# A second MLP product from fourteen block products a chunk instead of seven and four direct units

## The chip, the core and the metric

The kernel runs on one core of a Trainium2 chip. The metric is the device time of one execution in microseconds. All arithmetic is float32: each operand of a matmul is split into a high part (`wh`, rounded to the matmul's format) and a low part (`wl`, the rest), and a product of two matrices is three matmuls: high times high, high times low, low times high. The engines are TensorE (PE, with its weight loads PEld), VectorE (DVE), ScalarE (ACT), GpSimd (POOL) and SyncE (SP, which issues most transfers).

## The reference

Two residual layers over 256 positions of width 2048: the first mixes with a state-space scan, the second with a dilated attention; after each comes an MLP of width 8192:

```
def sq_relu_mlp(h, w1, w2):
    a = jax.nn.relu(h @ w1)
    return (a * a) @ w2
...
        x = x + sq_relu_mlp(rms_norm(x, norm_mlp[i]), mlp_w1[i], mlp_w2[i])
```

Here h is 256 x 2048, w1 is 2048 x 8192 and w2 is 8192 x 2048. The change touches only how `(a * a) @ w2` is computed.

## The kernel before

Every weight goes through the same three steps (`fetch`, L157): a transfer of 1 MB (128 x 2048 float32) into a buffer `raw`, a copy by ScalarE that rounds it to `wh` (L187), and a subtraction by VectorE that leaves `wl` (L188). Such a block is a unit. `unit_plan` (L47) lists all units in the order in which TensorE uses them, and `take` (L192) fetches two units ahead, since there are three buffers each of `raw`, `wh` and `wl`. In the MLP a unit's split is issued behind that of the unit before it (L178), so VectorE and ScalarE split in the plan's order. Each engine runs its own queue in order; a scheduler that works on its own estimate of time decides how the splits, the emptying of PSUM and the rest are interleaved on VectorE and ScalarE.

The MLP (`mlp`, L752) runs over the width 8192 in 8 chunks of 1024. In a chunk there are 8 U units of the first product: 32 matmuls each, half of them 512 and half 256 columns wide. A U unit ends in one PSUM bank and is emptied by `evacuate` (L773): ScalarE copies one half of the bank, VectorE adds the other (`cols_sum`, L235; in the trace the tile h_0t for U0, h_1t for U1), applies relu and the row factor (L777), ScalarE squares it and makes the high part, VectorE the low part.

While the U units of chunk c + 1 run, the second product of chunk c is worked off. Its left operand is 256 x 1024, seen as 2 x 2 blocks a11, a12 (the first 128 positions), a21, a22; its right one is 1024 x 2048. The columns of the result are four blocks of 512, j = 0 to 3. For j = 0 and 1 the 2 x 2 block product is made from seven products instead of eight (P1 to P7, Winograd's form): `combine` (L782) makes four combinations of the a blocks, and the weight blocks are combined by transfers that accumulate, which GpSimd issues (L176): they add the next block to the buffer `wa` or `wb` in place, once the split before has read it. A product is 12 matmuls of 512 columns (L812). It ends in a bank x, w or z, and VectorE adds that bank to the residual `x_res` or subtracts it (L818), with the running sums in the banks, so that seven products give all four blocks. For j = 2 and 3 the product is made directly, in four D units of 24 matmuls each (`rows_unit`, L238).

The order of a chunk is written by hand (L69):

```
CHUNK_ORDER = ("U0 U1 P1 U2 P2 U3 U4 P5 D20 D21 P3 U5 U6 P6 U7 D30 P7 D31 P4").split()
```

U and D units share four PSUM banks in turn, the products and small work the four others. Chunk 7 has no U units beside it and is multiplied directly.

Of the kernel before, what the change touches and what calls it, by code (L numbers as in the profile page):

```python
# [14 lines left out]
P = 128  # L15
S = 256
# [22 lines left out]
LOOKAHEAD = 3  # L39
# [7 lines left out]
def unit_plan():  # L47
# [21 lines left out]
CHUNK_ORDER = ("U0 U1 P1 U2 P2 U3 U4 P5 D20 D21 P3 U5 U6 P6 U7 D30 P7 D31 P4").split()  # L69
# [10 lines left out]
def mlp_plan(layer):  # L80
    plan = [("w1", layer, 0, u) for u in range(8)]
    for c in range(FC):
        if c + 1 < FC:
            for item in CHUNK_ORDER:
                if item[0] == "U":
                    plan.append(("w1", layer, c + 1, int(item[1])))
                elif item[0] == "P":
                    plan.append(("w2", layer, c, item))
                else:
                    plan.append(("w2", layer, c, int(item[1]), int(item[2])))  # L90
        else:
            plan += [("w2", layer, c, j, q) for j in range(4) for q in range(2)]
    return plan
# [3 lines left out]
def hybrid_trunk_kernel(ctx: ExitStack, tc: tile.TileContext, a: dict, out: bass.AP):  # L97
# [7 lines left out]

    def mm_bank(name):
        return psum.tile([P, 512], F32, tag="mm", name=name, bufs=4)

    def sm_bank(name):
        return psum.tile([P, 512], F32, tag="sm", name=name, bufs=4)  # L110
# [24 lines left out]
    def source(u):  # L135
        kind = u[0]
        if kind == "in":
            return a["w_in"][u[1] * 10 + u[2]], 2048
        if kind == "dt":
            return a["w_dt"], 2048  # L140
        if kind == "out":
            return a["w_out"][u[1] * 4 + u[2]], 2048
        if kind == "qk":
            return a["w_qk"][u[1] * 6 + u[2]], 2048
        if kind == "v":
            return a["w_v"][u[1] * 4 + u[2]], 1536
        if kind == "o":
            return a["w_o"][u[1] * 4 + u[2]], 2048
        if kind == "w1":
            return a["w1"][(u[1] * FC + u[2]) * 8 + u[3]], 2048  # L150
        if len(u) == 4:
            q, j = WINOGRAD[u[3]][1:3]
        else:
            j, q = u[3:]
        return a["w2"][((u[1] * FC + u[2]) * 4 + j) * 2 + q], 2048

    def fetch(i, ends=(16,)):  # L157

        src, n = source(plan[i])
        product = plan[i][3] if plan[i][0] == "w2" and len(plan[i]) == 4 else None  # L160
        where, _, _, begins = WINOGRAD.get(product, ("raw", 0, 0, True))
        if where == "raw":
            raw = wts.tile([P, 2048], F32, tag="raw", name=f"raw{i}", bufs=3)
        elif begins:
            raw = sums_of[where] = mlp_pool[0].tile([P, 2048], F32, tag=where, name=f"{where}{i}", bufs=1)
        else:
            raw = sums_of[where]
        wh = wts.tile([P, 2048], F32R, tag="wh", name=f"wh{i}", bufs=3)
        wl = wts.tile([P, 2048], F32R, tag="wl", name=f"wl{i}", bufs=3)
        ready[i] = (wh, wl)  # L170
        for k0, k1 in zip((0, *ends), ends):
            c = slice(k0 * n // 16, k1 * n // 16)
            if begins:
                load[i] = nc.sync.dma_start(raw[:, c], src[:, c]).ins
            else:
                nc.gpsimd.dma_start(raw[:, c], src[:, c], accum_op=ALU.add)  # L176
            with ExitStack() as order:
# [3 lines left out]
                if product == "P4":  # L181
# [10 lines left out]
    def take(*u):  # L192
# [3 lines left out]
        while cursor[1] < min(len(plan), i + LOOKAHEAD):  # L196
# [5 lines left out]
    def cols_units(us, xs, names, cuts=(), first=False, between=None):  # L202
# [3 lines left out]
        banks = [mm_bank(name) for name in names]  # L206
# [545 lines left out]
    def mlp(layer, pool, xn, done):  # L752
# [9 lines left out]
        mlp_pool[0] = pool  # L762

# [4 lines left out]
        def chunk(c):  # L768
            act = pool.tile([P, 8, 2, S], F32R, tag="act", name=f"act{layer}_{c}", bufs=2)
            r = pool.tile([P, 8, S], F32, tag="r", name=f"r{layer}_{c}", bufs=1)  # L770
            return act, r

        def evacuate(c, u, ps, act, r):  # L773
            name = f"h{layer}_{c}_{u}"
            tot = cols_sum(ps, name)
            t = r[:, u]
            nc.vector.scalar_tensor_tensor(t, tot, 0.0, rb, op0=ALU.max, op1=ALU.mult)  # L777
            nc.scalar.activation(t, t, AF.Square)  # L778
            nc.scalar.activation(act[:, u, 0, :], t, AF.Copy)
            nc.vector.tensor_tensor(act[:, u, 1, :], t, act[:, u, 0, :].bitcast(F32), ALU.subtract)  # L780

        def combine(c, r):  # L782

            t1, t2 = slice(0, P), slice(P, S)
            a11, a12, a21, a22 = r[:, :4, t1], r[:, 4:, t1], r[:, :4, t2], r[:, 4:, t2]
            s = [pool.tile([P, 4, P], F32, tag="s", name=f"s{layer}_{c}_{k}", bufs=2) for k in range(2)]
            parts = {}

            def split(k, t):
                parts[k] = pool.tile([P, 4, 2, P], F32R, tag=f"s{k}", name=f"sp{layer}_{c}_{k}", bufs=1)  # L790
                nc.scalar.activation(parts[k][:, :, 0], t, AF.Copy)
                nc.vector.tensor_tensor(parts[k][:, :, 1], t, parts[k][:, :, 0].bitcast(F32), ALU.subtract)

            nc.vector.tensor_tensor(s[0], a21, a22, ALU.subtract)
            split(1, s[0])
            nc.vector.scalar_tensor_tensor(s[1], s[0], -1.0, a11, op0=ALU.mult, op1=ALU.subtract)
            split(2, s[1])
            s4 = pool.tile([P, 4, P], F32, tag="s", name=f"s{layer}_{c}_3", bufs=2)
            nc.vector.scalar_tensor_tensor(s4, a12, -1.0, s[1], op0=ALU.mult, op1=ALU.subtract)
            split(4, s4)  # L800
            s3 = pool.tile([P, 4, P], F32, tag="s", name=f"s{layer}_{c}_2", bufs=2)
            nc.vector.tensor_tensor(s3, a11, a21, ALU.add)
            split(3, s3)
            return parts
# [11 lines left out]
        def put(m, j, ps, op):  # L816
            xc = x_res[:, m, j * 512:(j + 1) * 512]
            nc.vector.tensor_tensor(xc, xc, ps, op)  # L818

        act, r = chunk(0)  # L820
        us, names = [("w1", layer, 0, u) for u in range(8)], [f"h{layer}_0_{u}" for u in range(8)]
        for u, ps in enumerate(cols_many(us, xs, names)):
            evacuate(0, u, ps, act, r)

        for c in range(FC - 1):
            parts = combine(c, r)
            act_next, r_next = chunk(c + 1)
            banks = {}

            def half(k0, t):  # L830
                return lambda i, part: act[:, k0 + i, part, t]

            t1, t2 = slice(0, P), slice(P, S)
            of = {"P1": half(0, t1), "P2": half(4, t1), "P4": half(4, t2)}
            for k, item in ((1, "P5"), (2, "P6"), (3, "P7"), (4, "P3")):
                of[item] = lambda i, part, k=k: parts[k][:, i, part]
            lhs = lambda k, part, t: act[:, k, part, t]
            for item in CHUNK_ORDER:
                if item[0] == "U":
                    u = int(item[1])  # L840
                    ps = in_order(lambda: cols_units([("w1", layer, c + 1, u)], xs,
                                                     [f"h{layer}_{c + 1}_{u}"], first=(u == 0))[0])
                    evacuate(c + 1, u, ps, act_next, r_next)
                elif item[0] == "D":
                    j, q = int(item[1]), int(item[2])
                    if q == 0:
                        banks[j] = [mm_bank(f"d{layer}_{c}_{j}_{m}") for m in range(NH)]
                    in_order(lambda: rows_unit(banks[j], [("w2", layer, c, j, q)], lhs, 4 * q, 4, 512,
                                               q == 0, q == 1))
                    if q == 1:  # L850
                        add_residual(banks[j], j)
                else:
                    where = {"P1": "x", "P6": "x", "P7": "x", "P4": "x", "P5": "w", "P3": "w",
                             "P2": "z"}[item]
                    first = where not in banks
                    if first:
                        banks[where] = sm_bank(f"p{where}{layer}_{c}")
                    product(c, item, banks[where], of[item], first)
                    for m, j, op in {"P1": [(0, 0, ALU.add)], "P2": [(0, 0, ALU.add)],
                                     "P5": [(1, 1, ALU.add)], "P3": [(0, 1, ALU.subtract)],  # L860
                                     "P6": [(0, 1, ALU.subtract)], "P7": [(1, 1, ALU.add)],
                                     "P4": [(1, 0, ALU.subtract)]}[item]:
                        put(m, j, banks[where], op)
            act, r = act_next, r_next

        c = FC - 1
        lhs = lambda k, part, t: act[:, k, part, t]
# [18 lines left out]
    with tc.tile_pool(name="mlp1", bufs=1) as pool:  # L886
# [5 lines left out]
        def gained(j):  # L892
            if j == 0:
                fin.append(pool.tile([P, D], F32, tag="wb", name="fin", bufs=1))
# [116 lines left out]
```

## Time and profile before

| | |
|---|---|
| median of 3 runs | 2602.84 us (2599.51 to 2604.07) |
| the profiled execution | 2599.4 us |
| its span | 2597.6 us |
| MLP of the first layer | about 675 to 1386 us of the span |
| MLP of the second layer | about 1905 us to the end |
| PE, DVE, ACT busy over the span | 99%, 72%, 56% |
| mean moved by DMA | 206 GB/s |

Times of single instructions come from the profiled execution. Instructions that follow each other on an engine overlap a little in the records, so the sum of their durations is more than the time that they occupy. A line such as `wl<-raw,wh 128x2048 ... x13 | 29.8, 2291` is a group: what is written from what, the shape, how many, their busy time in us, and the mean of one in ns; behind the next bar stands how long the engine sat idle before them, and what ended that. In the list of a stretch by engines the columns are named in the text.

### The profile page before, as it was taken

Reading aid. Unit: us, or ns where it says so; the run is one execution under the profiler, and the core shown is the slowest. Engines: PE = TensorE matmul, PEld = TensorE weight load, DVE = VectorE, ACT = ScalarE, POOL = GpSimd, SP = SyncE. Lnnn points to the kernel's source line nnn. Section 1 sums busy time; section 2 is a strip of 40 time slices with the busy share of each in tenths; the row PEclk is TensorE's granted clock in tenths of the full one; section 3 lists DMA queues with packets and bytes.
Section 4 is the critical chain, followed back from the end, with each engine's and each line's share of the span. In section 5 each row is a group of like instructions: output and inputs, shape, how many; then the busy total and the mean of one; then the engine's idle time right before and its main releaser. Section 6 shows DMA issues by size and latency. Waiting matters only on the chain.

```text
span 2597.6 us, 34416 instructions
## 1 busy us (share of the span) xinstructions
PE 2582.3 (99%) x13977; PEld 2211.8 (85%) x13977; DVE 1878.7 (72%) x2182; ACT 1459.1 (56%) x1774; POOL 160.0 (6%) x131
## 2 busy tenths in 40 slices
PE   9999999999999999999999999999999999999998
PEld 7888888888888888888888999998888888888887
DVE  7888688686677677777766666666667777677765
ACT  7675365464555555555546655656565555555554
POOL 0121021211000000000000000000000000000001
PEclk9999999999999999999999999999999999999999
DMA  7645555555577787778765454444457777877783
GB/s 284 209 169 193 191 195 180 180 191 187 191 222 232 236 231 239 229 235 234 231 195 183 166 175 162 159 158 165 168 209 216 234 237 235 232 230 239 228 241 131
DMA packets 79087, 533.88 MB, mean 206 GB/s; under 512 B 8784, under 2 KB 9424, under 8 KB 19536
## 3 DMA queue, kind: packets, MB, share of 16 engines
q1 hardware_dynamic: 68256, 462.86, 50.5%
q0 software_dynamic: 8064, 58.72, 12.5%
q10 hardware_dynamic: 2608, 10.09, 1.2%
q8 instruction: 110, 1.80, 0.3%
q14 instruction: 49, 0.40, 0.0%
HBM read 529.48 MB, written 2.16 MB: 205 GB/s over the span
## 4 chain that ended last, share of the span: by engine, by line
PE 95%; DVE 2%; ACT 1%; DMA 1%; POOL 1%; issue 1%; SPq 0%; ACTq 0%; POOLq 0%; DVEq 0%
PE h L215 28%; PE qk L215 10%; PE c L215 8%; PE px L812 6%; PE d L249 5%; PE d L250 5%; PE d L251 5%; PE pw L812 3%; PE wo L250 2%; PE wo L249 2%; PE wo L251 2%; PE z L250 2%; PE z L251 2%; PE z L249 2%; PE v L249 2%; PE v L251 2%
## 5 line engine op out<-in xcount | busy, mean ns | idle before, releaser
L188 DVE TENSOR_TENSOR wl<-raw,wh 128x2048 fp32r<-128x2048 f32 (+4 forms) x428 | 934.6, 2185 | 578.0 <-ACT wh L187 577.0
L187 ACT ACTIVATE wh<-raw 128x2048 fp32r<-128x2048 f32 (+4 forms) x428 | 782.7, 1831 | 640.8 <-PE h L215 216.5
L215 PE MATMUL h<-xn,wh 128*128 128x512 f32 x2048 | 715.9, 394 | 0.0
L215 PE MATMUL h<-xn,wl 128*128 128x256 f32 x2048 | 571.2, 280 | 0.0
L215 PEld LDWEIGHTS h<-xn,wh 128*128 128x128 f32 x2048 | 383.9, 188 | 87.0
L215 PEld LDWEIGHTS h<-xn,wl 128*128 128x128 f32 x2048 | 383.6, 187 | 4.2
L215 PE MATMUL c<-xn,wh 128*128 128x512 f32 x768 | 272.4, 397 | 2.5 <-ACT wh L187 2.3
L215 PE MATMUL qk<-xn,wh 128*128 128x512 f32 x768 | 271.1, 395 | 0.0
L251 PE MATMUL d<-wh,act 128*128 128x512 f32 x576 | 224.3, 390 | 0.0
L250 PE MATMUL d<-wl,act 128*128 128x512 f32 x576 | 223.9, 389 | 0.0
L249 PE MATMUL d<-wh,act 128*128 128x512 f32 x576 | 218.7, 390 | 0.0
L215 PE MATMUL qk<-xn,wl 128*128 128x256 f32 x768 | 216.7, 284 | 0.0
L215 PE MATMUL c<-xn,wl 128*128 128x256 f32 x768 | 215.0, 282 | 0.8 <-DVE wl L188 0.8
L215 PEld LDWEIGHTS c<-xn,wh 128*128 128x128 f32 x768 | 143.7, 188 | 37.2 <-ACT wh L187 4.4
L215 PEld LDWEIGHTS qk<-xn,wh 128*128 128x128 f32 x768 | 143.9, 188 | 30.2
L215 PEld LDWEIGHTS c<-xn,wl 128*128 128x128 f32 x768 | 143.9, 188 | 3.0 <-DVE wl L188 1.1
L215 PEld LDWEIGHTS qk<-xn,wl 128*128 128x128 f32 x768 | 143.7, 188 | 3.2 <-issue 2.7
L251 PEld LDWEIGHTS d<-wh,act 128*128 128x128 f32 x576 | 108.1, 188 | 22.6
L249 PEld LDWEIGHTS d<-wh,act 128*128 128x128 f32 x576 | 108.1, 188 | 22.3
L250 PEld LDWEIGHTS d<-wl,act 128*128 128x128 f32 x576 | 108.1, 188 | 22.0
L778 ACT ACTIVATE r<-r 128x256 f32<-128x256 f32 x128 | 52.2, 410 | 101.7 <-DVE r L777 101.7
L250 PE MATMUL z<-wl,xn 128*128 128x512 f32 x256 | 101.4, 396 | 0.3 <-DVE wl L188 0.3
(348 smaller groups left out, 4186.3 us busy)
## 6 DMA issues: line engine op xcount, KB each, us to landing
raw<-in_w SPq DMA_DIRECT2D x214, 1024.0 KB, 4.9
raw<-in_w_in SPq DMA_DIRECT2D x74, 1024.0 KB, 4.8
raw<-in_w_qk SPq DMA_DIRECT2D x48, 1024.0 KB, 4.8
wa<-in_w POOLq DMA_DIRECT2D x42, 1024.0 KB, 8.2
raw<-in_w_out SPq DMA_DIRECT2D x32, 1024.0 KB, 4.8
raw<-in_w_v SPq DMA_DIRECT2D x32, 768.0 KB, 4.3
wa<-in_w SPq DMA_DIRECT2D x14, 1024.0 KB, 4.8
wb<-in_w SPq DMA_DIRECT2D x14, 1024.0 KB, 5.0
```

The costliest lines, as they stand in the source:

```text
L187: high[i] = nc.scalar.activation(wh[:, c], raw[:, c], AF.Copy).ins
L188: low[i] = nc.vector.tensor_tensor(wl[:, c], raw[:, c], wh[:, c].bitcast(F32), ALU.subtract).ins
L215: latest[0] = nc.tensor.matmul(ps[:, :n], (wh, wl)[part][:, kt * P:(kt + 1) * P], xs[:, kt, :, :].rearrange("p a t -> p (a t)")[:, :n], st ...
L249: nc.tensor.matmul(banks[m][:, :n], hi, wh[:, c], start=st, stop=False)
L250: nc.tensor.matmul(banks[m][:, :n], hi, wl[:, c], start=False, stop=False)
L251: latest[0] = nc.tensor.matmul(banks[m][:, :n], lo, wh[:, c], start=False, stop=sp).ins
L778: nc.scalar.activation(t, t, AF.Square)
L812: latest[0] = nc.tensor.matmul(ps, lhs(i, part), w[:, n], start=(first and i == 0 and part == 0 and w is wh), stop=(i == 3 and part == 1), ...
```

## The change

All four column blocks now go through seven products, in two halves: a for j = 0 and 1, b for j = 2 and 3. A chunk has 14 products (1a, 1b, 5a, ...) and no D units. The names are those of the products before without the P.

- The weight blocks are combined in buffers Aa, Ab, Ba, Bb. 1 loads A, 5 and 6 accumulate into it by transfers; for 4, VectorE adds to it the block that product 2 loads, which is on the chip (how = "sum"), and no transfer is made. 3 loads B, 7 accumulates into it.
- Product 2 of each half keeps its bank (za, zb) through all seven chunks and is added to the residual once. Products 1, 6, 7 and 4 share a bank x, 5 and 3 a bank w, in each half.
- There is a fourth pair of `wh` and `wl`, used in the chunks alone, and a unit is fetched as soon as the pair that was used longest ago is free. In the chunks the U units and product 2 have two `raw` buffers; the third is Aa.
- The eight PSUM banks are named singly. In the chunks the U units have banks 0 and 1, the products banks 2 to 7.
- Of the high and low parts of a, those of a21 are left out, since no product needs them; for chunk 7 `complete` makes them.
[...]

```diff
-CHUNK_ORDER = ("U0 U1 P1 U2 P2 U3 U4 P5 D20 D21 P3 U5 U6 P6 U7 D30 P7 D31 P4").split()
+CHUNK_ORDER = ("1a 1b U0 U1 U2 5a U3 5b 3a U4 3b U5 6a 6b 7a U6 7b 2a 4a U7 2b 4b").split()
...
-WINOGRAD = {
-    "P1": ("wa", 0, 0, True), "P2": ("raw", 1, 0, True), "P5": ("wa", 0, 1, False),
-    "P3": ("wb", 1, 1, True), "P6": ("wa", 1, 1, False), "P7": ("wb", 0, 1, False),
-    "P4": ("wa", 1, 0, False),
+PRODUCTS = {
+    "1": ("A", 0, 0, "load"), "5": ("A", 0, 1, "add"), "6": ("A", 1, 1, "add"), "4": ("A", 1, 0, "sum"),
+    "3": ("B", 1, 1, "load"), "7": ("B", 0, 1, "add"), "2": ("raw", 1, 0, "load"),
 }
...
+    class Slots:
...
+        def peek(self, among):
+            return next(k for k in self.order if k in among)
+
+        def use(self, k, i=None):
+            self.order.remove(k)
+            self.order.append(k)
+            self.user[k] = i
+            return k
+
+    banks_of, raws, splits = Slots(8), Slots(3), Slots(4)
+
+    def bank(name, among):
+        k = banks_of.use(banks_of.peek(among))
+        return psum.tile([P, 512], F32, tag=f"b{k}", name=name, bufs=1)
...
+    def chunked(i):
+        return plan[i][0] == "w1" and plan[i][2] > 0 or plan[i][0] == "w2" and len(plan[i]) == 4
+
+    def split_slot(i):
+        return splits.peek(range(4 if chunked(i) else 3))
...
         if where == "raw":
-            raw = wts.tile([P, 2048], F32, tag="raw", name=f"raw{i}", bufs=3)
+            k = raws.use(raws.peek(range(2 if chunked(i) else 3)))
+            raw = wts.tile([P, 2048], F32, tag=f"raw{k}", name=f"raw{i}", bufs=1)
...
+                if how == "sum":
+                    nc.vector.tensor_tensor(raw[:, c], raw[:, c], sums_of["raw" + item[1]][:, c], ALU.add)
                     high[i] = nc.scalar.activation(wh[:, c], raw[:, c], AF.Copy, scale=-1.0).ins
...
-        while cursor[1] < min(len(plan), i + LOOKAHEAD):
+        while cursor[1] < len(plan) and splits.user.get(split_slot(cursor[1]), -1) < i:
...
+                    ps = in_order(lambda: cols_units([("w1", layer, c + 1, u)], xs, [name],
+                                                     made=[bank(name, range(2))])[0])
+                    nxt.evacuate(u, ps)
+                    continue
+                key, m, j, op = put[item[0]]
+                key += item[1]
+                first = item[0] in "15" or item[0] == "2" and c == 0
+                if first:
+                    banks[key] = bank(f"p{key}{layer}_{c}", [place[key]])
+                product(c, item, banks[key], of[item[0]], first)
+                if item[0] != "2" or c == FC - 2:
+                    j += 2 * (item[1] == "b")
+                    xc = x_res[:, m, j * 512:(j + 1) * 512]
+                    nc.vector.tensor_tensor(xc, xc, banks[key], op)
...
-    nc = bacc.Bacc("TRN2", target_bir_lowering=False, num_devices=1)
+    nc = bacc.Bacc("TRN2", target_bir_lowering=False, num_devices=1, dynamic_dma_scratch_size=4096)
```

Where one chunk follows another, VectorE's queue read as follows before (first layer, from the split for P1 of chunk 2 to the residual addition that reads P1's bank, px0_2). wl161 is the split for P1, wl162 and wl163 those of U2 and P2, h0_3_0t and h0_3_1t are the additions that empty U0's and U1's banks.

```order
L188 TENSOR_TENSOR wl161_7665<-wa161_7663,wh161_7664 128x2048
L802 TENSOR_TENSOR s0_2_2_7656<-r0_2_7004 128x512
L792 TENSOR_TENSOR sp0_2_4_7653<-s0_2_3_7651,sp0_2_4_7653 128x4x128
L188 TENSOR_TENSOR wl162_7712<-raw162_7710,wh162_7711 128x2048
L235 TENSOR_TENSOR h0_3_0t_7704<-h0_3_0_7669,h0_3_0x_7702 128x256
L792 TENSOR_TENSOR sp0_2_3_7658<-s0_2_2_7656,sp0_2_3_7658 128x4x128
L777 SCALAR_TENSOR_TENSOR r0_3_7662<-h0_3_0t_7704,xn1rb_5941 128x256
L188 TENSOR_TENSOR wl163_7760<-raw163_7758,wh163_7759 128x2048
L235 TENSOR_TENSOR h0_3_1t_7751<-h0_3_1_7716,h0_3_1x_7749 128x256
L818 TENSOR_TENSOR x_res_69<-x_res_69,px0_2_7757 128x512
```

Between a product's split and the addition that reads its bank stood two further splits, and U0's addition stood directly behind the split of U2.

After the change VectorE's queue reads, at the same place one chunk earlier: the residual additions that read 4b (pxb0_0) and 1a (pxa0_1), the first combinations of a (L852, L854), and the splits of 1b (wl144, from Ab), U0 (wl145) and U1 (wl146).

```order
L902 TENSOR_TENSOR x_res_69<-x_res_69,pxb0_0_6372 128x512
L852 TENSOR_TENSOR ssq_junk_75<-r0_1_6351 128x512
L821 TENSOR_TENSOR a20_1_6350<-r0_1_6351,a20_1_6350 128x256
L854 SCALAR_TENSOR_TENSOR s0_1_6990<-ssq_junk_75,r0_1_6351 128x512
L902 TENSOR_TENSOR x_res_69<-x_res_69,pxa0_1_7010 128x512
L222 TENSOR_TENSOR wl144_6955<-Ab144_6953,wh144_6954 128x2048
L222 TENSOR_TENSOR wl145_6973<-raw145_6971,wh145_6972 128x2048
L222 TENSOR_TENSOR wl146_7013<-raw146_7011,wh146_7012 128x2048
```

The addition that reads 1a's bank now stands directly ahead of the split of 1b, which TensorE uses directly behind 1a. The same stands at all 12 places where a chunk of products follows another.

The queue goes on with splits of the combined operands (L849), the addition that reads 1b, the splits of U2 (wl147) and 5a (wl148, from Aa), and the addition that empties U0's bank (h0_2_0t):

```order
L849 TENSOR_TENSOR sp0_1_5_6992<-ssq_junk_75,sp0_1_5_6992 128x4x128
L849 TENSOR_TENSOR sp0_1_6_6996<-s0_1_6990,sp0_1_6_6996 128x4x128
L902 TENSOR_TENSOR x_res_69<-x_res_69,pxb0_1_7030 128x512
L856 SCALAR_TENSOR_TENSOR ssq_junk_75<-r0_1_6351,s0_1_6990 128x512
L858 TENSOR_TENSOR s0_1_6990<-r0_1_6351 128x512
L849 TENSOR_TENSOR sp0_1_3_7000<-ssq_junk_75,sp0_1_3_7000 128x4x128
L222 TENSOR_TENSOR wl147_7033<-raw147_7031,wh147_7032 128x2048
L849 TENSOR_TENSOR sp0_1_7_7004<-s0_1_6990,sp0_1_7_7004 128x4x128
L222 TENSOR_TENSOR wl148_7052<-Aa143_6906,wh148_7051 128x2048
L269 TENSOR_TENSOR h0_2_0t_7090<-h0_2_0_7050,h0_2_0x_7088 128x256
```

U0's addition has moved behind the splits of U2 and of 5a.

More of the change, by code (lines that the diff above doesn't have):

```diff
@@ L38 @@
 FC = 8
-LOOKAHEAD = 3
 def alibi_slope(g, h):
@@ L104, in hybrid_trunk_kernel, with __init__ @@
     dram = ctx.enter_context(tc.tile_pool(name="dram", bufs=1, space=bass.MemoryType.DRAM))
+    class Slots:
+        def __init__(self, n):
+            self.order, self.user = list(range(n)), {}
+        def peek(self, among):
[9 more added lines that the diff above has]
+        return psum.tile([P, 512], F32, tag=f"b{k}", name=name, bufs=1)
     def mm_bank(name):
-        return psum.tile([P, 512], F32, tag="mm", name=name, bufs=4)
+        return bank(name, range(4))
     def sm_bank(name):
-        return psum.tile([P, 512], F32, tag="sm", name=name, bufs=4)
+        return bank(name, range(4, 8))
     x_res = const.tile([P, NH, D], F32, name="x_res")
@@ L172, in fetch @@
             c = slice(k0 * n // 16, k1 * n // 16)
-            if begins:
+            if how == "load":
                 load[i] = nc.sync.dma_start(raw[:, c], src[:, c]).ins
-            else:
+            elif how == "add":
                 nc.gpsimd.dma_start(raw[:, c], src[:, c], accum_op=ALU.add)
@@ L200, in take, with cols_units @@
         return ready.pop(i)
-    def cols_units(us, xs, names, cuts=(), first=False, between=None):
+    def cols_units(us, xs, names, cuts=(), first=False, between=None, made=None):
         ws = [take(*u) for u in us]
-        banks = [mm_bank(name) for name in names]
+        banks = made or [mm_bank(name) for name in names]
         ends = (0, *cuts, KT)
@@ L766, in in_order @@
                 return make()
[L768 to L804, printed above, removed]
@@ new lines, in mlp, with __init__, evacuate, complete @@
+        class Chunk:
+            def __init__(self, c):
+                name = f"{layer}_{c}"
+                self.c = c
+                self.a1 = [pool.tile([P, 4, 2, P], F32R, tag="a1", name="a1" + name, bufs=2)]
+                self.a2 = pool.tile([P, 4, 2, S], F32R, tag="a2", name="a2" + name, bufs=2)
+                self.r = pool.tile([P, 8, S], F32, tag="r", name="r" + name, bufs=1)
+            def evacuate(self, u, ps):
+                tot = cols_sum(ps, f"h{layer}_{self.c}_{u}")
+                t = self.r[:, u]
+                nc.vector.scalar_tensor_tensor(t, tot, 0.0, rb, op0=ALU.max, op1=ALU.mult)
+                nc.scalar.activation(t, t, AF.Square)
+                a, t = (self.a1[0][:, u], t[:, left]) if u < 4 else (self.a2[:, u - 4], t)
+                nc.scalar.activation(a[:, 0], t, AF.Copy)
+                nc.vector.tensor_tensor(a[:, 1], t, a[:, 0].bitcast(F32), ALU.subtract)
+            def complete(self):
+                a = pool.tile([P, 4, 2, P], F32R, tag="Bb", name=f"a1r{layer}_{self.c}", bufs=1)
+                t = self.r[:, :4, right]
+                nc.scalar.activation(a[:, :, 0], t, AF.Copy)
+                nc.vector.tensor_tensor(a[:, :, 1], t, a[:, :, 0].bitcast(F32), ALU.subtract)
+                self.a1.append(a)
+            def plain(self, k, part, t):
+                if k < 4:
+                    return self.a1[t.start // P][:, k, part]
+                return self.a2[:, k - 4, part, t]
+            def combine(self):
+                r, c = self.r, self.c
+                a11, a12, a21, a22 = r[:, :4, left], r[:, 4:, left], r[:, :4, right], r[:, 4:, right]
+                even = ssq_junk.rearrange("p (k t) -> p k t", k=4)
+                odd = pool.tile([P, 4, P], F32, tag="s", name=f"s{layer}_{c}", bufs=1)
+                of = {"1": lambda i, part: self.a1[0][:, i, part],
+                      "2": lambda i, part: self.a2[:, i, part, left],
+                      "4": lambda i, part: self.a2[:, i, part, right]}
+                def split(item, t):
+                    sp = pool.tile([P, 4, 2, P], F32R, tag="s" + item, name=f"sp{layer}_{c}_{item}", bufs=1)
+                    nc.scalar.activation(sp[:, :, 0], t, AF.Copy)
+                    nc.vector.tensor_tensor(sp[:, :, 1], t, sp[:, :, 0].bitcast(F32), ALU.subtract)
+                    of[item] = lambda i, part: sp[:, i, part]
+                nc.vector.tensor_tensor(even, a21, a22, ALU.subtract)
+                split("5", even)
+                nc.vector.scalar_tensor_tensor(odd, even, -1.0, a11, op0=ALU.mult, op1=ALU.subtract)
+                split("6", odd)
+                nc.vector.scalar_tensor_tensor(even, a12, -1.0, odd, op0=ALU.mult, op1=ALU.subtract)
+                split("3", even)
+                nc.vector.tensor_tensor(odd, a11, a21, ALU.add)
+                split("7", odd)
+                return of
@@ L814, in product @@
                             stop=(i == 3 and part == 1), skip_group_check=True).ins
[L816 to L820, printed above, removed]
+        cur = Chunk(0)
         us, names = [("w1", layer, 0, u) for u in range(8)], [f"h{layer}_0_{u}" for u in range(8)]
         for u, ps in enumerate(cols_many(us, xs, names)):
-            evacuate(0, u, ps, act, r)
-        for c in range(FC - 1):
[L826 to L837, printed above, removed]
+            cur.evacuate(u, ps)
@@ L838, in mlp @@
+        banks = {}
+        put = {"1": ("x", 0, 0, ALU.add), "6": ("x", 0, 1, ALU.subtract), "7": ("x", 1, 1, ALU.add),
+               "4": ("x", 1, 0, ALU.subtract), "5": ("w", 1, 1, ALU.add), "3": ("w", 0, 1, ALU.subtract),
+               "2": ("z", 0, 0, ALU.add)}
+        place = {"wa": 2, "wb": 3, "xa": 4, "xb": 5, "za": 6, "zb": 7}
+        for c in range(FC - 1):
+            of = cur.combine()
+            nxt = Chunk(c + 1)
             for item in CHUNK_ORDER:
                 if item[0] == "U":
-                    u = int(item[1])
@@ L841, in mlp @@
[L841 to L863, printed above, removed]
@@ L864, in mlp @@
-            act, r = act_next, r_next
+                    u, name = int(item[1]), f"h{layer}_{c + 1}_{item[1]}"
+                    ps = in_order(lambda: cols_units([("w1", layer, c + 1, u)], xs, [name],
[5 more added lines that the diff above has]
+                first = item[0] in "15" or item[0] == "2" and c == 0
@@ L866, in mlp @@
+                if first:
[5 more added lines that the diff above has]
+                    nc.vector.tensor_tensor(xc, xc, banks[key], op)
+            cur = nxt
         c = FC - 1
-        lhs = lambda k, part, t: act[:, k, part, t]
+        cur.complete()
@@ L868, in mlp @@
+        lhs = cur.plain
         for j in range(4):
```

33 lines of the change are left out of this document (20 added, 13 removed).

## The prediction

> **What bounds the kernel now.** I read part 1 of the page first, then TensorE's own waits, then the chain that ended last.
>
> ```profile
> span 2597.6 us, 34416 instructions
> ...
> PE 2582.3 (99%) x13977; PEld 2211.8 (85%) x13977; DVE 1878.7 (72%) x2182; ACT 1459.1 (56%) x1774; POOL 160.0 (6%) x131
> ```
>
> ```profile
> PE c L215 <- ACT wh L187: 2.3, 2, 1.5
> ...
> PE z L250 <- DVE wl L188: 0.3, 1, 0.3
> ```
>
> ```profile
> 859.65 2.75 PE pw L812 x12
> 862.40 0.23 PE d L249
> ...
> 876.00 11.17 PE h L215 x64
> ...
> 945.26 2.75 PE pw L812 x12
> ```
>
> TensorE is busy for all but 15 us. The longest and the shortest of its listed waits are shown; none lies in an MLP. In the MLPs the chain is TensorE alone: a block product of 12 matmuls takes 2.75 us, so 0.229 us for a matmul; two U units take 11.17, so 5.59 each. One chunk lasts 945.26 - 859.65 = 85.61 us. The next view is one such chunk by engine (TensorE, weight loads, VectorE, ScalarE, GpSimd, then granted clock, DMA share, GB/s):
>
> ```profile
> 1016.96:1102.57 85.61, 85.61 (x437) 72.90 (x437) 62.53 (x63) 46.78 (x48) 3.45 (x4) 1.00 0.79 234
> ```
>
> VectorE has 23 us to spare in a chunk and the DMA engines a fifth. This is the cover under which the new work must fit.
>
> **The change, part by part.** *Matmuls removed.* Before, a chunk's second product is 7 block products of 12 matmuls and 4 D units of 24: 180. After, it is 14 of 12: 168. There are 7 such chunks in each of two layers, so 14 x 12 x 0.229 = 38.5 us leave the path. All of it is a gain only if TensorE still never waits.
>
> *Work added.* Units per chunk go from 8 + 7 + 4 = 19 to 8 + 14 = 22, each with a ScalarE and a VectorE split; VectorE also makes two sums of 128x2048 and one more addition to the residual.
>
> ```profile
> L188 DVE TENSOR_TENSOR wl<-raw,wh 128x2048 fp32r<-128x2048 f32 x13 | 29.8, 2291 | 20.5 <-ACT wh L187 20.5
> L780 DVE TENSOR_TENSOR act<-r,act 128x256 fp32r<-128x256 f32 x9 | 3.8, 418 | 0.0
> L792 DVE TENSOR_TENSOR sp<-s,sp 128x512 fp32r<-128x512 f32 x4 | 2.7, 683 | 0.0
> ...
> L187 ACT ACTIVATE wh<-raw 128x2048 fp32r<-128x2048 f32 x14 | 26.8, 1917 | 26.7 <-PE h L215 14.6 <-PE d L251 8.9 <-issue 2.9
> ```
>
> The sums are priced at the split's row (two operands and a result of the same size). VectorE per chunk: 24 x 2.29 for splits and sums, at most 24 x 0.42 for what empties the U units, 20 x 0.68 for the combination and the residual: 78.6 us. But these durations overlap at their ends:
>
> ```profile
> 1080.13 0.68 DVE L796 SCALAR_TENSOR_TENSOR s<-s,r 128x512 f32<-128x512 f32 x1
> 1080.73 0.69 DVE L256 TENSOR_TENSOR x_res<-d,x_res 128x512 f32<-128x512 f32 x1
> ...
> 1082.53 2.28 DVE L188 TENSOR_TENSOR wl<-raw,wh 128x2048 fp32r<-128x2048 f32 x1
> 1084.73 0.69 DVE L799 SCALAR_TENSOR_TENSOR s<-r,s 128x512 f32<-128x512 f32 x1
> ```
>
> A 128x512 instruction occupies 0.60 us, a split 2.20 us, and by the same 0.08 a 128x256 one 0.33. With 68 instructions that is 78.6 - 68 x 0.08 = 73 us against a TensorE chunk of 85.61 - 2.75 = 82.9 us. On average VectorE fits. What matters is where its queue, which runs in order, makes TensorE wait.
>
> *First wait: product 1b.* On TensorE 1b follows 1a directly. On VectorE, in the order shown above, the residual addition that reads 1a's result stands directly ahead of 1b's split. Take zero at the end of 1a's last matmul. The delays from one engine to the next:
>
> ```profile
> 1044.12 0.39 PE L251 MATMUL d<-wh,act 128*128 128x512 f32 x1
> ```
>
> ```profile
> 1044.54 0.69 DVE L256 TENSOR_TENSOR x_res<-d,x_res 128x512 f32<-128x512 f32 x1 [0.26 <-PE d L251]
> ```
>
> ```profile
> 26.59 1.23 DVE L188 TENSOR_TENSOR wl<-raw,wh 128x1024 fp32r<-128x1024 f32 x1
> ...
> 27.87 0.38 PE L215 MATMUL c<-xn,wl 128*128 128x256 f32 x1 [0.76 <-DVE wl L188]
> ```
>
> A matmul's end (1044.12 + 0.39) reaches VectorE 0.03 later; a split's end (26.59 + 1.23) reaches TensorE 0.05 later. So the addition starts at 0.03, 1b's split at 0.63; it ends at 2.92 and 1b's second matmul, the first that reads wl, starts at 2.97. Unhindered it would start at 0.07 (a last matmul starts 0.39 before its end, and two starts further is 0.458 later). The wait is 2.90 us, whatever the transfers do.
>
> 1b's weights go into the buffer that 4b's split reads last, so their load starts after it.
>
> ```profile
> 1016.88 1.92 ACT L187 ACTIVATE wh<-raw 128x2048 fp32r<-128x2048 f32 x1 [1.54 <-PE h L215]
> ```
>
> ```profile
> 1063.78 2.28 DVE L188 TENSOR_TENSOR wl<-wb,wh 128x2048 fp32r<-128x2048 f32 x1
> ```
>
> ```profile
> 1066.10 0.33 SPq L174 DMA_DIRECT2D wb<-in_w  x1
> ```
>
> I count from the end of U5. U6's split waits for U5's buffer and ScalarE's 1.92, so it starts at about 2.05. From there VectorE is full: by the occupancies above, 7b's split starts at 5.5, 2a's at 8.3, the sum for 4a at 10.5; ScalarE reads the sum at 12.8, so 4a's split starts at 14.8; U7's at 17.6, 2b's at 20.1, the sum for 4b at 22.3, 4b's split at 26.6, ending at 28.9. SyncE issues the load 0.04 later (1063.78 + 2.28 to 1066.10). 1a ends three products, U6, three products, U7 and three products after U5: 9 x 2.75 + 2 x 5.59 + 0.16 = 36.1. So the load leaves at -7.2. What a load takes:
>
> ```profile
> q1 hardware_dynamic: 2168, 15.75, 51.6%
> q0 software_dynamic: 576, 4.19, 26.7%
> ...
> raw<-in_w SPq DMA_DIRECT2D x14, 1024.0 KB, 4.9
> wa<-in_w POOLq DMA_DIRECT2D x3, 1024.0 KB, 8.2
> ```
>
> Two stretches of the same chunk, 1024.8 to 1031 and 1051.8 to 1059, each hold one load issued beside an accumulating transfer:
>
> ```profile
> raw<-in_w SPq DMA_DIRECT2D x1, 1024.0 KB, 6.9
> ```
>
> ```profile
> raw<-in_w SPq DMA_DIRECT2D x1, 1024.0 KB, 6.1
> ```
>
> Alone, 1b's load lands at -2.3 and is split by ScalarE in time. Beside 5a's accumulation, which starts some 2 us after it, it lands up to -0.3, ScalarE ends at 1.6, and the wait grows to 3.9. I take 3.2, nearer to the lower end, since only part of the load has company.
>
> *Second wait: U2.* U units now have two PSUM banks instead of a share in four, so U2 writes the bank of U0 and needs VectorE's addition h_0t done. In the order this stands behind the splits of U2 and 5a. From the same zero: 1b's split 0.63, U0's 2.83, U1's 5.03; five instructions of 0.60 and one more split of an operand reach 11.0. U2's load needs the staging buffer that U0's split frees at 5.1; with two instead of three staging buffers it can't be earlier. It lands at 10.1 if it takes 4.9 and at 12.0 if 6.8; it runs beside the accumulation for 5b, which starts after 1b's split, so I take 6.6, near the 6.9 row. With ScalarE's 1.92, U2's split starts between 12.1 and 14.0; then 2.20, 0.60, 2.20 and 0.42 + 0.05: U2 may start between 17.5 and 19.4. TensorE is there at 2.97 + 11 x 0.229 + 2 x 5.59 = 16.7. The wait is 0.8 to 2.75 us; I take 2.6. If the load were no limit, the queue alone would let U2 start at 16.5: no wait.
>
> Both occur where one chunk follows another, 6 times in a layer. The first chunk of a layer has 1b's weights loaded early and h_0t behind U3's split at a moment when VectorE has room. So 12 x (3.2 + 2.6) = 69.6 us.
>
> *The rest.* The last chunk: U7's result is made behind two further splits, and TensorE can fill in only part with other matmuls: 0 to 3 us a layer, I take 1.5, so 3. The extra accumulations (6 instead of 4) cost GpSimd 2 issues and are needed 20 us later. The four shorter splits of a1 and the sum that TensorE now keeps in PSUM for product 2 save VectorE time where it isn't needed. The single names of the banks leave the rotation outside the MLP as it was, but shuffle some matmuls in the first two groups of the first layer: -3 to 3, I take 0.
>
> The sum, against the profiled execution's 2599.4: 2599.4 - 38.5 + 69.6 + 3 = 2633.5. The median of the runs is 3.4 above that execution, so about 2635. Ends: 12 x (2.9 + 0.8) gives 2606, 12 x (3.9 + 2.75) with 3 us more in each layer gives 2650.
>
> [...] A granted clock of 1.00 stands in the chunk's row above, where TensorE has no gap. [...]
>
> **Rivals.** *The splits stay ahead* (faster). If the fourth pair of split buffers lets VectorE finish 1b's split before 1a ends, neither wait is there: 2599.4 - 38.5 + 3 = 2564. For it: 73 us of work in 83. Against it: the order, in which 1b's split can't pass the addition. It decides at 38.5 / 12 = 3.2 us of waiting per boundary: below that, the change is faster. Chance 0.15, with the partial cases.
>
> *Only 1b waits* (same). Loads land in 4.9 and U2's bank is free in time: 2599.4 - 38.5 + 12 x 2.9 + 3 = 2599. Chance 0.15.
>
> *Transfers become the limit* (slower). By the two queue rows a load is 0.516 x 85.61 / 15 = 2.95 us of all engines, an accumulation 0.267 x 85.61 / 4 = 5.7: 14 and 6 of them are 75.5 us of 82.9, 91% after 79%. If loads at both places land 1.2 us later still: 2635 + 12 x 2.4 = 2664. Chance 0.09.
>
> *The clock drops after each wait* (slower). At half the clock the 2.75 us after each of 24 waits double: 2635 + 66 = 2701. The chunk's row has 1.00 throughout, so nothing here speaks for it. Chance 0.06. [...]
>
> **How the numbers follow.** The forecast, both waits at every boundary, has 0.55. Its own range is 2606 to 2650. The range of 8 in 10 takes in the case of one wait and most of the transfers' case: 2597 to 2660. About 0.2% is what a measurement of this kernel can tell from no change. Faster 0.15; same 0.15; slower 0.55 + 0.09 + 0.06 = 0.70.
>
> **What would show it.** In the profile after, TensorE should wait about 3 us for wl before product xb, 12 times, and 1 to 3 us for h_0t before a U unit, 12 times; a chunk should last near 89 us, with VectorE full from U6 to 1b. No such waits, or a chunk of 83, would make the forecast wrong; so would waits in other places, before 4a, 4b or 5b, where I found 1.5 us or more to spare.

## The result, and the profile after

| | median of the runs | profiled execution |
|---|---|---|
| before | 2601.18 us (2598.84 to 2604.07) | 2599.4 us |
| after | 2688.89 us (2687.53 to 2689.68) | 2688.71 us |

The ratio is 1.0336, 95% interval 1.0318 to 1.0354: slower, by 88 us. The forecast was slower at 2635 us, with a range up to 2660. Direction and places were right, the size was not, and the time lies outside the range.

Part 1 of the page after, to be held against that of before (2597.6 us, TensorE 2582.3 us busy):

```profile
span 2686.9 us, 34258 instructions
...
PE 2590.4 (96%) x13809; PEld 2205.8 (82%) x13809; DVE 2035.5 (76%) x2272; ACT 1522.7 (57%) x1814; POOL 190.3 (7%) x159
```

168 matmuls have gone, yet TensorE is busy 8 us longer, and it stands still for 2686.9 - 2590.4 = 96.5 us instead of 15.3. So there are two losses: time in which TensorE waits, and time in which it works but slowly. TensorE's own waits (line and tile, what it waited for, us in total, times, longest) show the first:

```profile
PE h L249 <- DVE h_0t L269: 48.2, 14, 5.6
PE pxb L868 <- DVE wl L222: 29.7, 12, 2.7
...
PE pxb L868 <- ACT wh L221: 2.6, 2, 1.4
```

These are the two forecast places: 1b waits for its split, U2 for the addition h_0t that empties U0's bank. 12 and 14 times is once at each of 12 boundaries between chunks, and for U2 once more in the first chunk of each layer. The chain of waits across one boundary (start, us, what):

```profile
923.69 0.04 DVE x_res L902
...
924.30 1.01 DVE wl L222
925.30 1.20 issue
926.50 2.29 DVE wl L222
928.79 0.02 issue
928.81 9.85 DMA raw<-in_w
...
938.74 1.92 ACT wh L221
940.67 0.02 issue
940.69 0.55 DVE wl L222
...
943.50 2.28 DVE wl L222
945.78 0.35 DVE h_0t L269
946.13 0.04 issue
946.18 5.99 PE h L249 x25
```

Read it downwards: the addition that reads 1a's result, 1b's split behind it, U0's split, and only then, at 928.81, can U2's load leave, since U0's split frees its staging buffer. The load takes 9.85 us; at the six boundaries of the first layer this step is 8.4 to 10.0 us long, where the forecast had 6.6. Then come ScalarE's part, U2's split, one more split (5a's) and h_0t. TensorE starts U2 at 946.18, 5.6 us late.

The second loss is in the granted clock. Four stretches of 3.4 us directly behind such waits, from the list of stretches on TensorE (the stretch; its length; busy time and matmuls; granted clock; DMA share; GB/s):

```profile
834.57:838.00 3.43, 3.43 (x16) 1.00 0.54 60
852.76:856.20 3.44, 3.44 (x13) 0.60 0.93 205
946.18:949.60 3.42, 3.42 (x12) 0.58 0.86 187
1019.82:1023.20 3.38, 3.38 (x10) 0.63 0.58 70
```

The first is behind 1b's wait at one boundary, the last behind 1b's wait at another; the two between are behind U2's. The clock records of the profiles before and after hold two values only, 1.00 (full clock) and 0.50 (half clock); 0.58 to 0.63 stands for a stretch with some of each. U2 is slow at each of the 12 boundaries: its first 12 matmuls take 3.4 to 4.0 us instead of 2.2. 1b is slow at 7 of the 12: there the 11 matmuls behind its wait take 3.8 to 4.2 us instead of 2.6. From one boundary to the next, here from U3 to the next U3, it now takes 93.2 us (columns: TensorE, weight loads, VectorE, ScalarE, GpSimd, clock, DMA share, GB/s):

```profile
862.91:956.10 93.19, 84.95 (x426) 71.59 (x425) 73.38 (x69) 51.55 (x50) 5.20 (x6) 0.98 0.78 226
```

Before it was 85.61. VectorE is busy for 73.4 of it, the DMA engines for 78%: neither is full.

### The profile page after: what moved, and what is told of

The parts are those of the page before. It is cut to its first block, busy times and chain, and to the rows that moved or that the text cites. A ratio compares the mean times of both kernels' runs of the same rounds, so it can differ in the third digit from the quotient of the medians.

```text
span 2686.9 us, 34258 instructions
## 1 busy us (share of the span) xinstructions
PE 2590.4 (96%) x13809; PEld 2205.8 (82%) x13809; DVE 2035.5 (76%) x2272; ACT 1522.7 (57%) x1814; POOL 190.3 (7%) x159
## 3 DMA queue, kind: packets, MB, share of 16 engines
q8 instruction: 108, 1.77, 0.3%
## 4 chain that ended last, share of the span: by engine, by line
PE 83%; DVE 6%; DMA 6%; issue 3%; ACT 2%; POOL 0%; SPq 0%; ACTq 0%; POOLq 0%; DVEq 0%
PE h L249 21%; PE qk L249 10%; PE c L249 10%; DMA raw<-in_w 5%; PE pxa L868 5%; DVE wl L222 4%; PE pxb L868 4%; PE pwb L868 3%; PE pwa L868 3%; PE wo L284 2%; PE wo L283 2%; PE wo L285 2%; PE z L284 2%; PE z L285 2%; PE z L283 2%
## 5 line engine op out<-in xcount | busy, mean ns | idle before, releaser
L222 DVE TENSOR_TENSOR wl<-raw,wh 128x2048 fp32r<-128x2048 f32 (+4 forms) x386 | 838.5, 2177 | 386.8 <-ACT wh L221 385.9
L221 ACT ACTIVATE wh<-raw 128x2048 fp32r<-128x2048 f32 (+4 forms) x386 | 700.1, 1819 | 426.4 <-PE wo L285 81.6
L249 PE MATMUL h<-xn,wh 128*128 128x512 f32 x2048 | 744.8, 404 | 48.2 <-DVE h_0t L269 48.2
L249 PE MATMUL h<-xn,wl 128*128 128x256 f32 x2048 | 583.6, 285 | 0.0
L249 PEld LDWEIGHTS h<-xn,wh 128*128 128x128 f32 x2048 | 396.5, 194 | 144.7 <-DVE h_0t L269 52.6
L222 DVE TENSOR_TENSOR wl<-Ab,wh 128x2048 fp32r<-128x2048 f32 x42 | 96.0, 2287 | 33.3 <-ACT wh L221 33.3
L221 ACT ACTIVATE wh<-Ab 128x2048 fp32r<-128x2048 f32 x42 | 80.3, 1912 | 53.2 <-PE h L249 41.5
L283 PE MATMUL z<-wh,xn 128*128 128x512 f32 x256 | 101.8, 398 | 0.0
L285 PE MATMUL z<-wh,xn 128*128 128x512 f32 x256 | 101.4, 396 | 0.0
L283 PE MATMUL wo<-wh,y3t 128*128 128x512 f32 x256 | 100.1, 392 | 0.0
L284 PE MATMUL wo<-wl,y3t 128*128 128x512 f32 x256 | 100.0, 391 | 0.0
```

The source lines that it names most:

```text
L221: high[i] = nc.scalar.activation(wh[:, c], raw[:, c], AF.Copy).ins
L222: low[i] = nc.vector.tensor_tensor(wl[:, c], raw[:, c], wh[:, c].bitcast(F32), ALU.subtract).ins
L249: latest[0] = nc.tensor.matmul(ps[:, :n], (wh, wl)[part][:, kt * P:(kt + 1) * P], xs[:, kt, :, :].rearrange("p a t -> p (a t)")[:, :n], st ...
L283: nc.tensor.matmul(banks[m][:, :n], hi, wh[:, c], start=st, stop=False)
L284: nc.tensor.matmul(banks[m][:, :n], hi, wl[:, c], start=False, stop=False)
L285: latest[0] = nc.tensor.matmul(banks[m][:, :n], lo, wh[:, c], start=False, stop=sp).ins
```

## The experiments

Theory: each boundary loses time by order, in three parts: 1b's wait, U2's wait, and half clock behind the waits. Rival: VectorE and the transfers as a whole have too much to do, so that a wait removed here comes back elsewhere. All edits are on the changed kernel unless said; all times are medians, those of before beside them 2599.8 to 2600.0 us.

### 1b behind U0

```
-CHUNK_ORDER = ("1a 1b U0 U1 U2 5a U3 5b 3a U4 3b U5 6a 6b 7a U6 7b 2a 4a U7 2b 4b").split()
+CHUNK_ORDER = ("1a U0 1b U1 U2 5a U3 5b 3a U4 3b U5 6a 6b 7a U6 7b 2a 4a U7 2b 4b").split()
```

> Only the order of a chunk is changed: 1b stands behind U0 instead of ahead of it. The theory (the boundary loses time by the order of the splits: 2.9 us at 1b because its split stands behind the residual addition of 1a in VectorE's queue, 5 to 6 us at U2 because its load lands late beside two other transfers, and some 2 us of half clock behind that gap): with 18 us of U0 between 1a and 1b the wait at 1b is gone, and U2's split has more time, so 4 to 9 us of every one of the 12 boundaries come back: about 2580 to 2640 us. The rival (VectorE and the transfers as a whole have too much to do in a chunk, whatever the order): the wait moves to another place, and the time stays at 2680 to 2700 us.

Measured 2571.24 us, ratio to before 0.9891 (0.9875 to 0.9908): 118 us less than the changed kernel, below every expectation, and 29 us less than before. Both waits are gone. Part 1, TensorE's longest wait in an MLP, one chunk by engines, and the chain at a boundary:

```profile
PE 2550.9 (99%) x13809; PEld 2180.3 (85%) x13809; DVE 2031.3 (79%) x2272; ACT 1515.5 (59%) x1814; POOL 189.1 (7%) x159
```

```profile
PE h L249 <- DVE h_1t L269: 1.5, 4, 0.6
```

```profile
830.00:913.00 83.00, 83.00 (x427) 70.59 (x426) 72.97 (x69) 50.93 (x51) 5.18 (x6) 1.00 0.87 254
```

```profile
909.35 2.72 PE pxa L868 x12
912.07 5.59 PE h L249 x32
917.66 2.75 PE pxb L868 x12
```

This chunk is TensorE alone, 83.0 us; the others take up to 83.9. VectorE does the same work as in the changed kernel and the DMA share is higher, so the rival is out: the work fits, its order did not. Two rows of SyncE and VectorE tell why one place in the order is enough for both waits:

```profile
909.56 0.33 SPq L207 DMA_DIRECT2D raw<-in_w  x1
```

```profile
912.71 2.28 DVE L222 TENSOR_TENSOR wl<-Ab,wh 128x2048 fp32r<-128x2048 f32 x1
```

1b's split still stands behind the addition, but ends at 915.0, and TensorE comes to 1b at 917.7 only. And since the splits follow the plan, U0's is now made ahead of 1b's, before 1a ends at about 912.1. U2's load leaves 2.5 us before that moment, where it left 5.1 us behind 1a's end in the changed kernel (928.81 against 923.67). It still takes 8.5 to 9.3 us to land, and that no longer matters.

### Without the accumulation for 5b

```
-            elif how == "add":
+            elif how == "add" and item != "5b":
```

> The accumulating transfer that prepares the block sum for 5b is left out (so 5b, and what is built on its sum, multiply by sums that lack a block); the matmuls and splits are as many as in the changed kernel. The theory (U2's load lands 8.4 to 10 us after its issue because a second load and this accumulation share the DMA engines with it): U2's load lands 1.5 to 3 us earlier, the gap ahead of U2 falls from 5 to 6 us to 2 to 4, and with it some of the half clock behind it: about 2630 to 2665 us. The rival (the landing time is set by the queue of loads alone, not by the accumulation): landings stay at 8.4 to 10 us, and the time at 2685 to 2690 us.

Measured 2652.33 us (2645.92 to 2661.32), within the theory's range. At the boundary that answers to the one above, SyncE issues U2's load and ScalarE can start on it:

```profile
920.84 0.33 SPq L207 DMA_DIRECT2D raw<-in_w  x1
```

```profile
925.79 1.92 ACT L221 ACTIVATE wh<-raw 128x2048 fp32r<-128x2048 f32 x1 [5.57 <-DMA raw<-in_w]
```

That is 4.9 us from issue to landing instead of 9.85, with the next load close behind it in both kernels. At 11 of the 12 boundaries the load takes 4.7 to 4.9 us here, at one 5.9. So the second load alone does not make it late. In the kernel with 1b behind U0, U2's load has 5a's accumulation beside it and the next load only in its last 0.7 to 1.6 us, and takes 8.5 to 9.3 us: it is the accumulation. TensorE's waits:

```profile
PE pxb L868 <- DVE wl L222: 29.2, 12, 2.6
PE h L249 <- DVE h_0t L269: 20.1, 11, 4.5
```

1b waits as before; U2's wait falls from 48.2 to 20.1 us. What is left, some 1.7 us at a boundary, is mostly the queue. The edit has also changed VectorE's order: at 10 of the 12 boundaries h_0t now stands behind three splits, those of U2, 5a and U3, so the gain may be smaller than what the late load costs.

### A third bank for the U units

```
-        place = {"wa": 2, "wb": 3, "xa": 4, "xb": 5, "za": 6, "zb": 7}
+        place = {"wa": 2, "wb": 3, "xa": 4, "xb": 5, "za": 6, "zb": 6}
...
-                                                     made=[bank(name, range(2))])[0])
+                                                     made=[bank(name, (0, 1, 7))])[0])
```

The bank comes from product 2, which is added to the residual in every chunk, as in the kernel before.

> The U units get a third PSUM bank (0, 1 and 7), for which the two halves of product 2 are no longer kept in PSUM but added to the residual in every chunk (some more VectorE work, the same result). The theory (U2 waits for h_0t, the activation that frees bank 0 and stands behind the splits of U2 and 5a in VectorE's queue): U2 now waits for its own split alone, which ends 3 us ahead of h_0t, so the gap falls to about 2.6 us, too short for a half clock: 4 to 5 us at each of 12 boundaries, about 2630 to 2645 us. The rival (h_0t is late because VectorE is full, so what is saved at U2 is lost a unit later): 2680 to 2695 us.

Measured 2628.58 us, 60 us less than the changed kernel and a little below the theory's range:

```profile
PE pxb L868 <- DVE wl L222: 27.9, 12, 2.4
PE h L249 <- DVE wl L222: 7.4, 7, 1.8
```

U2 waits for its own split now, 7.4 us in all instead of 48.2. So the two-bank limit is what turned the late load into a long wait, by way of h_0t. That a gap of 2.6 us is too short for half clock, as the expectation has it, was assumed and is shown by no run: in this kernel half clock follows 1b's gaps, none longer than 2.41 us, at 7 boundaries.

### TensorE kept busy in the waits

Two kernels add matmuls. The first puts 24 between U1 and U2:

```
+                    if u == 2 and c > 0:
+                        fill = bank(f"fill{layer}_{c}", [2])
...
+                            for k in range(24):
```

> Work is added: 24 matmuls into an idle PSUM bank, results unused, stand between U1 and U2 in every chunk but the first, inside the time in which TensorE waits for U2's split. The theory (behind a gap of 5 to 6 us TensorE's clock is granted at about 0.6 for some 3 us, which costs 1.6 to 2.8 us at each boundary): the gap left is under 1 us, U2's 32 matmuls take 5.6 us again instead of 7.2 to 8.5, and 12 boundaries give back 19 to 30 us: about 2660 to 2670 us. The rival (U2's first matmuls are slow for another reason, such as reads beside the splits, or the slow stretch is covered by the next wait): U2 keeps its 7.2 us or more, and the time stays at 2686 to 2692 us.

Measured 2691.47 us. That lies in the rival's range, but not for the rival's reason: U2 is at full clock, as the theory had it, and 1b is now slow at 10 boundaries instead of 7. One boundary in the chain:

```profile
834.29 4.29 PE pxb L868 x11
838.59 11.25 PE h L249 x64
849.84 5.46 PE fill L893 x24
855.30 5.58 PE h L249 x32
```

```profile
PE h L249 <- DVE h_0t L269: 4.2, 2, 2.6
```

U2's 32 matmuls take 5.58 us, but 1b's 11 take 4.29 where 2.5 is full speed. And my sum was wrong: the filling takes 12 x 5.46 = 65.5 us, while the waits that it stands in were 48.2 - 4.2 = 44. It added 21.5 us, and that hid what the clock gave back. The second kernel therefore adds 11 matmuls ahead of 1b too:

```
+                if item == "1b" and c > 0:
+                    fill = bank(f"fillb{layer}_{c}", [3])
...
+                        for k in range(11):
```

> Work is added to the kernel with matmuls between U1 and U2: 11 more matmuls into another idle PSUM bank, results unused, ahead of 1b in every chunk but the first, inside the 2.5 us in which TensorE waits there. The theory (a gap of 2.5 us can already bring half clock: there 1b's 12 matmuls took 4.2 to 5.3 us at 10 of 12 boundaries instead of 2.8, in all about 22 us): 1b runs at full clock at every boundary and nothing else changes, so the 2691 us of the kernel with one filling falls by 15 to 22 us, to 2669 to 2677 us. The rival (1b's matmuls are slow because VectorE and ScalarE work beside them, not because TensorE stood still): they stay slow, and the time is 2688 to 2695 us.

Measured 2675.31 us, as the theory expected: 13.6 us less than the changed kernel, although TensorE has 420 matmuls more to do. Part 1:

```profile
PE 2647.2 (99%) x14229; PEld 2256.8 (84%) x14229; DVE 2035.5 (76%) x2272; ACT 1522.6 (57%) x1814; POOL 189.7 (7%) x159
```

The mean granted clock is 0.999 (changed kernel: 0.983). At 5.46 / 24 the 420 matmuls are 95.6 us; without them TensorE is busy for 2551.6 us. The kernel with 1b behind U0, which hardly waits, has 2550.9 for the same matmuls. So the changed kernel's 2590.4 us hold 39 us of slow clock. The difference between those two kernels' spans, 118.3 us, is 96.5 - 17.7 = 78.8 of standing still and 2590.4 - 2550.9 = 39.5 of slow work.

### The addition behind 1b's split

```
+                    with ExitStack() as late:
+                        if item == "1a":
+                            late.enter_context(tc.issue_after(low[cursor[0]]))
+                        nc.vector.tensor_tensor(xc, xc, banks[key], op)
```

> Only VectorE's order at 1b is changed: the addition to the residual that reads 1a's result stands behind 1b's split instead of ahead of it. The theory of the prediction (1b's wait is made by this order alone): the split starts as soon as ScalarE's part is done, and the wait all but goes; 12 x 2.6 us, and U2's load starts earlier by as much: about 2640 us. What the profile of the changed kernel says instead (1b's load lands so late that ScalarE's part ends 0.8 us ahead of the moment at which the split starts now): the wait falls by 0.8 us only, from 2.6 to 1.8, which is short enough to keep the clock up behind most of these gaps; 12 x (0.8 + about 1) less: about 2665 to 2675 us. If the order has nothing to do with it: 2686 to 2692 us.

Measured 2685.53 us: 3 us less, less than the scatter of these runs (2681.17 to 2687.52), and in none of the expected ranges; the nearest is that of an order without effect.

```profile
PE h L249 <- DVE h_0t L269: 54.3, 14, 7.3
PE pxb L868 <- DVE wl L222: 21.9, 12, 1.8
```

1b's wait falls by 0.65 us a boundary only. The addition was not the only thing ahead of that split: its weights come from a load that leaves after 4b's split, and in the changed kernel ScalarE's part of it ended at 923.44, only 0.9 us ahead of the split's start at 924.30:

```profile
921.52 1.92 ACT L221 ACTIVATE wh<-Ab 128x2048 fp32r<-128x2048 f32 x1 [0.69 <-DMA Ab<-in_w]
```

U2 then waits 6 us longer in all, so most of the little gain is given back: the addition now stands ahead of U0's split, and U2's load, which waits for that split, leaves at most 0.3 us earlier behind 1a's end. That a gap of 1.8 us keeps the clock up behind most of 1b's waits was right: the matmuls behind it take 2.62 to 2.67 us at 8 boundaries, and 3.73 to 4.22 us at the other 4. Shortening 1b's wait alone is worth almost nothing here, while shortening U2's alone, by the third bank, was worth 60 us.

### The banks' names alone, in the kernel before

```
-        return psum.tile([P, 512], F32, tag="mm", name=name, bufs=4)
+        return bank(name, range(4))
```

> The kernel before with one part of the change alone: its eight PSUM banks are named singly and taken in rotation, instead of four buffers in each of two groups. The prediction's term (0, between -3 and 3 us): 2597 to 2603 us. The first section of the changed kernel's profile ended 2.9 us later than that of the kernel before; if the names of the banks are the cause, this kernel is slower by about 3 us: 2602 to 2605 us. A rival for those 2.9 us, that they come from the loads for the MLP or from the scatter between executions, expects no difference.

Measured 2601.12 us, ratio 1.0005 (0.9996 to 1.0014): no difference that can be measured. That in the changed kernel's profile the first U unit starts at 697.4 instead of 694.5 us is not explained by this run's time: its interval reaches from 1 us less to 3.6 us more, so it can neither show nor exclude 2.9 us. In this run's own profile the first U unit starts at 699.2, and in those of all eight kernels with the new chunk at 696.2 to 697.7. Every profile with named banks thus has the later start; that the names cause it is not shown.

### Three pairs of split buffers, with 1b behind U0

```
-        return splits.peek(range(4 if chunked(i) else 3))
+        return splits.peek(range(3))
```

> The kernel with 1b behind U0, but with three pairs of split buffers in the chunks instead of four. If the fourth pair is what lets the splits run ahead where three products follow one another (VectorE needs 2.2 us for a split and 0.3 to 0.7 for each instruction between, TensorE 2.75 for a product), TensorE waits again in every chunk, 1 to 4 us: 2585 to 2625 us. If the order of the units was all that was wrong, three pairs do as well as four: 2569 to 2575 us.

Measured 2583.72 us, ratio to before 0.9938 (0.9924 to 0.9951): between the two expectations. The fourth pair is worth 12.5 us. TensorE's longest wait shows where most of that goes:

```profile
PE pxa L868 <- DVE wl L217: 8.3, 14, 0.6
```

This is 4a, once in every chunk, whose split comes after the sum made on VectorE.

## Why the prediction was wrong, point by point

**The saving was right.** 168 matmuls were to bring a chunk from 85.61 to 82.9 us where TensorE never waits; with 1b behind U0 it is 83.0 to 83.9. (Of the 38.5 us in all, that kernel keeps 29 against the one before; the rest is not resolved.) VectorE's 73 us and the 91% of DMA time in such a chunk came out at 72.97 us and 87%.

**The first wait was right in place and nearly in size**: 3.2 us taken, (29.7 + 2.6) / 12 = 2.7 measured. "Whatever the transfers do" was wrong: with the addition out of the way, 1b's load, which leaves only behind 4b's split, still makes TensorE wait 1.8 us.

**The second wait was right in place and too small.** 2.6 us taken, 2.75 as the upper end. Without the two first chunks (2.24 and 1.61 us, where I expected none) it is 44.4 / 12 = 3.7 us. The step that failed is the load's landing: "I take 6.6, near the 6.9 row". That row's load ran beside its accumulation for only 3.4 of its 6.9 us (1029.48 to 1032.90, where the accumulation landed); U2's load at the boundary shown runs beside the one for 5b for 8.2 of its 9.85 us (928.81 to 936.98). 8.4 to 10.0 us is what it took here, and without the accumulation 4.9. As an estimate from the two, each microsecond of overlap lengthens a load by some 0.6 us beyond the 4.9. Both waits together were 80.5 us where the sum had 69.6: 11 us of the miss. The direction was no luck, since the waits alone are more than the 38.5 us saved.

**The clock was the larger failure.** The sum had no term for it, and as a rival it got 0.06 and lay outside the range. It cost 39 us of the 55 by which the sum (2633.5) missed the profiled execution (2688.71). (The clock records agree: in the MLPs they have half clock in 19 stretches, 81.9 us in all, in which TensorE is busy for 71.8; half of that is 36 us.) The reason given was "The chunk's row has 1.00 throughout, so nothing here speaks for it". But that row has no gap in it, so it could not speak against it either: with gaps forecast at 24 places and no row showing what follows one, the cost should have been bounded between 0 and the rival's 66 us and the bound put into the range. With half of the 66 in the sum the forecast would have been 2668.

**The clock behind a gap, as these runs show it.** In the changed kernel 1b's gaps, none over 2.8 us long, brought half clock at 7 of 12 boundaries and left the clock at 1.00 at the other 5. Two gaps of the kernel with the addition behind the split, of which the longer one left it at 1.00:

```profile
850.77 0.50 PE L249 MATMUL h<-xn,wh 128*128 128x512 f32 x1 [3.48 <-DVE h_0t L269]
...
1016.32 0.80 PE L868 MATMUL pxb<-wl,a 128*128 128x512 f32 x1 [1.82 <-DVE wl L222]
```

The clock records of the changed kernel and of four of the experiments (no accumulation for 5b, third bank, one filling, addition behind the split) show more: in the MLPs every stretch of half clock, 62 in all, begins on a grid of 3.413 us that runs on through the execution. These are windows of that grid around the two gaps (the window; its length; TensorE's busy time and matmuls; granted clock; DMA share; GB/s):

```profile
845.66:849.07 3.41, 1.64 (x10) 1.00 0.01 5
849.07:852.48 3.41, 1.71 (x9) 1.00 0.94 317
852.48:855.90 3.42, 3.42 (x21) 1.00 0.98 182
1012.91:1016.32 3.41, 1.58 (x7) 1.00 1.05 219
1016.32:1019.73 3.41, 3.41 (x8) 0.50 0.67 94
```

The gap of 3.48 us is cut by an edge of the grid, with 1.77 us idle in one window and 1.70 in the next, and no half clock follows. The gap of 1.82 us lies in one window, and the next window is at half clock. In the five traces, without their first 200 and last 20 us, half clock followed each of the 54 full-clock windows in which TensorE stood idle for more than 1.87 us, none of the 60 with 1.0 to 1.73 us, and 8 of the 11 between. So in these traces half clock goes with the idle time within one window of the grid, and about half a window of it is enough. This is read off the traces; no run moved a gap against the grid. As an estimate from these numbers, a gap of less than 1.73 us brings no half clock, one of more than twice 1.87, 3.74 us, always does, and between them it depends on where the grid cuts it.

**The rest.** The banks' names: 0 taken; the run's interval leaves room for up to 3.6 us. What is left of the miss, 55 - 39 - 11 = 5 us, includes the first section's 2.9 us and is not resolved.

## What to carry to other kernels

When work is packed so tightly that a queue in order decides, ask for every unit where its load can leave, not only how long it takes: here one entry of the order, moved by one place, made the same work 118 us faster. A wait on TensorE that can fill more than half of a window of the 3.413 us grid seen here is to be priced with the slow stretch behind it (39 us over 19 such places here, some 2 us each), and a row without gaps is no evidence that this costs nothing. A load that shares the DMA engines with an accumulating transfer for most of its time should be given twice its time alone (8.4 to 10.0 us against 4.9 here), or an earlier start.

## What was not expected of the hardware

- A 1 MB load landed after 4.9 us with another load behind it, and after 8.4 to 10.0 us when an accumulation ran beside it as well.
- The length of a gap on TensorE does not decide alone whether the clock falls: 1.82 us brought it to 0.50 once, 3.48 us left it at 1.00 once, and of 1b's gaps of 1.8 to 2.8 us in the changed kernel 7 of 12 brought it down. What decides in these traces is how much of one window of a 3.413 us grid is idle, with the limit near half of it (between 1.73 and 1.87 us). The slow stretch lasts one window (14 of 19 places in the changed kernel) or two (the other 5).
- A filling that kept the clock up for U2 left 1b slow at 10 boundaries instead of 7. At the two boundaries where 1b stayed at full clock, its gap was cut by the grid (1.50 and 1.00 us idle in the two windows at one, 1.35 and 1.20 at the other); at the ten others one window had 1.96 us or more.
